# Memory cross-attention of an encoder layer: token and probability tiles split before the transposition, and transposed by DMA instead of by TensorE

## The chip, the cores and the metric

The kernel runs on one core of a Trainium2 chip, as one launch. The metric is the device time of that core in microseconds (us), the median over several executions. The core has five engines with instruction queues of their own: TensorE (PE in the profile; its weight loads are PEld), VectorE (DVE), ScalarE (ACT), GpSimd (POOL) and SyncE (SP, whose queue here issues almost all DMA transfers).

## The reference

One post-norm encoder layer over 1024 tokens of width 1024: a token mixer (an mLSTM in both directions beside a two-dimensional neighbourhood attention), a cross-attention into 256 memory tokens, and a gated convolutional feed-forward block, each followed by a residual sum and a layer norm. The change lies in the cross-attention alone:

```
def memory_xattn(x, mem, w_q, w_kv, w_o, b_o):
    q = (x @ w_q).reshape(b, t, 4, 256)
    k, v = split(mem @ w_kv)                      # 256 memory tokens, 4 heads x 256
    s = einsum('bthd,bmhd->bhtm', q, k) * 256 ** -0.5
    p = softmax(s, axis=-1)
    o = einsum('bhtm,bmhd->bthd', p, v).reshape(b, t, d)
    return o @ w_o + b_o
h = layer_norm(ALPHA * h + memory_xattn(h, ...), ln2_w, ln2_b)
```

## The kernel before

All large products are made of three float16 products. An operand is scaled by a power of two and written as a pair hi + lo, where hi is its value rounded to float16 and lo is the float16 of what is left. `split16` (L203 to L205) makes such a pair: ScalarE writes hi (L204) and VectorE writes lo (L205). `mm3` (L224 to L227) then issues hi x hi, hi x lo and lo x hi into the same PSUM bank, as lines L225, L226 and L227.

The weights of the cross-attention are folded early in the kernel: w_q with the keys of each head becomes `Kq` (1024 x 1024: token width by 4 heads x 256 memory tokens), and the values of each head with w_o become `Vo` (1024 x 1024). So a tile of 128 tokens needs two products of 128 x 1024 x 1024. Both contract over the partition axis, so the left operand of each has to be turned from token-major (tokens on the partitions) to token-minor (tokens along the row).

The 1024 tokens are eight tiles of 128, taken in the order of the list `todo`. The stages around the change are:

- The output projection of the mixer (`out_half`, with `after1`, L1296 to L1307) ends with layer norm 1 of each tile. Its tiles are stored to `h1_d` in DRAM (L1300). Here the first two tiles are already transposed for the attention (`to_hT` at L1304 and L1306).
- `to_hT` (L1265 to L1271) takes a tile `r`, a 128 x 1024 float32 array. TensorE transposes its eight 128 x 128 blocks, four to a PSUM bank (L1270), and `split16` evicts each bank as a pair of 128 x 512 into `h1T`.
- `scores` (L1386 to L1407) multiplies `h1T` with `Kq` (48 matmuls of 128 x 512), takes the row maximum of each head (L1396, L1397), the exponential with its row sum (L1400), the reciprocal (L1403), and multiplies the probabilities of each head with it in place (L1405). There is one buffer `P` of 128 x 1024 float32.
- `to_PT` (L1409 to L1418) transposes the eight blocks of `P` by TensorE (L1416) and evicts them with `split16` into a float16 pair. These pairs live in the tiles `vec0`, `vec1`, `vec2` of the pool `vecs`; `vec0` and `vec1` held the weight and the bias of layer norm 1 before (L1298 reads `vec0`, L1299 reads `vec1`).
- `out_d` (L1420 to L1435) multiplies the probabilities with `Vo` (48 matmuls), adds the residual (L1428), normalises, stores the tile to `h2_d` (L1431), and calls `to_B`, which transposes the tile once more by TensorE (L1332) for the feed-forward block. `to_B` is not touched by the change.

The loop at L1442 to L1451 runs `scores(n + 1)`, `to_PT(n)`, the load of tile n + 2 from `h1_d` (L1384), `to_hT(n + 2)`, and `out_d(n - 1)`. GpSimd adds the bias `b_xo` to tile n + 2 in place (L1449), after the tile's transposition has read it. The last three tiles' `out_d` is interleaved with the preparation of the first feed-forward weights (L1555 to L1578), whose loads (L1487) go into buffers that take the memory of the attention's work pool `ck` when that is closed (L1453).

Each engine runs its own instructions in a fixed order, SP's queue too: an instruction that waits holds all that stand behind it on the same engine. That order is fixed when the program is built, by a scheduler that works with estimated durations (`schedule_with_timeline_sim=True`). It is not simply the order of the source: in the trace the transpositions of one tile lie between matmuls of another.

Of the kernel before, what the change touches and what calls it, by code (L numbers as in the profile page):

```python
# [11 lines left out]
F16 = mybir.dt.float16  # L12
I32 = mybir.dt.int32
AF = mybir.ActivationFunctionType
OP = mybir.AluOpType
PSUM = bass.MemoryType.PSUM

D = 1024
# [38 lines left out]
def encoder(ctx, tc, I, out):  # L57
    nc = tc.nc
    V, A, G, T, S = nc.vector, nc.scalar, nc.gpsimd, nc.tensor, nc.sync
# [25 lines left out]
    def tbank():  # L85
        return pp.tile([128, 512], F32, name="tp", tag="tp", bufs=2).rearrange("p (k t) -> p k t", k=4)
# [17 lines left out]
    ident = consts.tile([128, 128], F32, name="ident")  # L104
# [98 lines left out]
    def split16(hi, lo, src, s):  # L203
        A.activation(hi, src, AF.Copy, scale=s)  # L204
        return V.scalar_tensor_tensor(lo, src, s, hi, op0=OP.mult, op1=OP.subtract)  # L205
# [76 lines left out]
    with ExitStack() as ca:  # L282
# [819 lines left out]
        with ExitStack() as cn:  # L1102
# [4 lines left out]
            o = 0  # L1107
# [27 lines left out]
            def na_gen():  # L1135
                n = 0
                for p in range(4):
# [15 lines left out]
                    for cb in range(4):  # L1153
# [26 lines left out]
                        for g in range(4):  # L1180
# [4 lines left out]
                                kl[:, r0:r0 + R, :].rearrange("p r c -> p (r c)"), True, True)  # L1185
                            P = nw.tile([128, 384], F32, name="P", tag="P", bufs=5)
                            mn = nw.tile([128, 2], F32, name="mn", bufs=6)
                            V.tensor_tensor_reduce(P[:, :nk], ps, tabs[ct, rt].rearrange("p r c -> p (r c)"), 1.0, BIG,
                                                   OP.add, OP.min, mn[:, 0:1])
                            A.activation(P[:, :nk], P[:, :nk], AF.Exp, scale=-1.0, bias=mn[:, 0:1],  # L1190
                                         accum_out=mn[:, 1:2])
                            V.reciprocal(mn[:, 1:2], mn[:, 1:2])
                            V.tensor_scalar(P[:, :nk], P[:, :nk], mn[:, 1:2], None, op0=OP.mult)
                            yield 1
# [38 lines left out]
    with ExitStack() as cb_:  # L1233
# [27 lines left out]
        rs, hT, probs, rq, holds, stores = {}, {}, {}, [], [], []  # L1261
        cC = ExitStack()
        ck = cC.enter_context(tc.tile_pool(name="wkC", bufs=1, reuse_waits="tile"))

        def to_hT(ck, n, r):  # L1265
            hT[n] = ck.tile([128, 2, 8, 128], F16, name="h1T", tag="h1T", bufs=2)
            for q in range(2):
                pt = tbank()
                for k in range(4):
                    T.transpose(pt[:, k, :], r[:, (4 * q + k) * 128:(4 * q + k + 1) * 128], ident)  # L1270
                split16(hT[n][:, 0, 4 * q:4 * q + 4], hT[n][:, 1, 4 * q:4 * q + 4], pt, s1)  # L1271

        with ExitStack() as cB:
            wk = cB.enter_context(tc.tile_pool(name="wkB", bufs=1, reuse_waits="tile"))
            lw, lb = vec(0, "ln1_w"), vec(1, "ln1_b")
            p1, s1 = pow2(ln_bound(lw, lb)[1], 14)
# [109 lines left out]
        def scores(ck, n):  # L1386
            t = hT.pop(n)
            P = ck.tile([128, D], F32, name="P", tag="P", bufs=1)
            mn = small.tile([128, 8], F32, name="mn", bufs=3)
            for ch in range(2):  # L1390
                ps = bank("S2")
                for k in range(8):
                    c = slice(ch * 512, ch * 512 + 512)
                    mm3(ps, t[:, 0, k], t[:, 1, k], Kq[0][:, k, c], Kq[1][:, k, c], k == 0, k == 7)
                m = mn[:, 2 * ch:2 * ch + 2]
                V.tensor_reduce(m, ps.rearrange("p (h m) -> p h m", h=2), axis=mybir.AxisListType.X, op=OP.max)  # L1396
                V.tensor_scalar(m, m, ncs, None, op0=OP.mult)  # L1397
                for h in range(2 * ch, 2 * ch + 2):
                    o = h % 2 * 256
                    A.activation(P[:, h * 256:h * 256 + 256], ps[:, o:o + 256], AF.Exp, scale=cs_, bias=mn[:, h:h + 1],  # L1400
                                 accum_out=mn[:, 4 + h:5 + h])
                l = mn[:, 4 + 2 * ch:6 + 2 * ch]
                V.reciprocal(l, l)  # L1403
                for h in range(2 * ch, 2 * ch + 2):
                    V.tensor_scalar(P[:, h * 256:h * 256 + 256], P[:, h * 256:h * 256 + 256], mn[:, 4 + h:5 + h], None,  # L1405
                                    op0=OP.mult)
            return P  # L1407

        def to_PT(P, n):  # L1409
            i = 2 if n == NT - 1 else n % 2  # L1410
            t = f16(vecs.tile([128, D], F32, name=f"vec{i}", tag=f"vec{i}")).rearrange(
                "p (n k t) -> p n k t", n=2, k=8)
            for q in range(2):
                pt = tbank()
                for k in range(4):
                    T.transpose(pt[:, k, :], P[:, (4 * q + k) * 128:(4 * q + k + 1) * 128], ident)  # L1416
                split16(t[:, 0, 4 * q:4 * q + 4], t[:, 1, 4 * q:4 * q + 4], pt, 2.0 ** 14)
            probs[n] = t  # L1418

        def out_d(n, lag=1):  # L1420
# [20 lines left out]
        P = scores(ck, 0)  # L1441
        for n in range(NT - 1):  # L1442
            Pn = scores(ck, n + 1)
            to_PT(P, n)
            P = Pn
# [4 lines left out]
            if 0 < n < NT - 2:  # L1450
                run(out_d(n - 1))  # L1451
        to_PT(P, NT - 1)
        cC.close()  # L1453

# [143 lines left out]
        with ExitStack() as cE:  # L1598
# [113 lines left out]
            for v in range(NFF):  # L1712
# [25 lines left out]
                if v == NFF - 2:  # L1738
                    y_scale(0)
                    s1 = sy[0][1]  # L1740
# [41 lines left out]
        with ExitStack() as cF:  # L1782
# [49 lines left out]
            for tt in range(NT):  # L1832
                load_r(tt + 2)
                r = rs.pop(tt)
# [8 lines left out]
                n = 256 if last else 512  # L1843
# [95 lines left out]
```

## Time and profile before

| | us |
|---|---|
| median of 3 runs | 1519.65 |
| lowest and highest | 1518.59, 1522.79 |
| span of the profiled execution | 1519.5 |
| PE busy | 1457.8 (96%) |
| DVE busy | 1030.0 (68%) |
| ACT busy | 821.2 (54%) |
| POOL busy | 570.6 (38%) |
| attention stage (first scores to last `out_d` matmul) | 669.7 to 858.1 |

The profiled execution has no other time than its span. It is 0.15 us below the median. The page groups instructions by source line, so L225, L226 and L227 stand for the three products of all matmuls that go through `mm3`; the names beside them (`S<-kq,h1T` for the scores, `S<-whi,vec` and `S<-wlo,vec` for `out_d`) tell which product it is. A matmul's row gives its full duration, but matmuls overlap: the time that one takes away from the next is the distance between their starts.

### The profile page before, as it was taken

How to read it: one execution, taken by the hardware profiler on the slowest of the kernel's cores; microseconds unless marked ns; L12 is line 12 of the kernel's file. 1: busy time of each engine (PE TensorE's matmuls, PEld its weight loads, DVE VectorE, ACT ScalarE, POOL GpSimd, SP SyncE). 2: the span in 40 equal slices, each digit the busy share in tenths (PEclk: the TensorE clock that was granted, in tenths of full speed). 3: DMA queues.
4: the chain of work that ended last, by engine and by line, in shares of the span. 5: the costliest groups of instructions: out<-in, count | busy, mean ns of one | idle time of the engine just before them, and what ended most of it. 6: DMA issues, size and time to landing. Idle time of an engine off the chain costs nothing.

```text
span 1519.5 us, 21884 instructions
## 1 busy us (share of the span) xinstructions
PE 1457.8 (96%) x8188; PEld 881.0 (58%) x8188; DVE 1030.0 (68%) x1953; ACT 821.2 (54%) x1385; POOL 570.6 (38%) x453
## 2 busy tenths in 40 slices
PE   8999999999999898998999989999999999999998
PEld 7998766456766887864555434444444444444444
DVE  7868766536677678575357778887787779707434
ACT  5766565655544666333245767777777767503000
POOL 5442357303325765043112364444443420300543
PEclk9999999999999999999999989999999999999999
DMA  8846653215545533553011242223222436712121
GB/s 305 326 156 211 189 190 120 91 54 144 155 118 180 196 124 131 213 194 125 29 42 60 96 152 112 111 111 125 111 111 111 152 125 222 276 43 89 51 82 56
DMA packets 84895, 208.61 MB, mean 137 GB/s; under 512 B 7091, under 2 KB 36019, under 8 KB 81462
## 3 DMA queue, kind: packets, MB, share of 16 engines
q1 hardware_dynamic: 84496, 206.46, 39.2%
q8 instruction: 64, 1.05, 0.3%
q0 software_dynamic: 144, 0.49, 0.2%
q14 instruction: 41, 0.34, 0.1%
q10 hardware_dynamic: 150, 0.27, 0.0%
HBM read 158.34 MB, written 49.35 MB: 137 GB/s over the span
## 4 chain that ended last, share of the span: by engine, by line
PE 48%; DVE 18%; ACT 9%; DMA 9%; issue 4%; POOL 2%; SPq 1%; DVEq 0%; ACTq 0%; POOLq 0%
PE dn L225 5%; PE dn L227 5%; PE dn L226 5%; DMA sv<-in_w_down_dram 5%; PE S L225 3%; PE S L227 3%; PE S L226 3%; DVE wlo L205 3%; DVE cbuf L1617 3%; DVE cbuf L1618 2%; PE cl L225 2%; PE cl L226 2%; PE cl L227 2%; PE cu L227 1%; PE o L1202 1%
## 5 line engine op out<-in xcount | busy, mean ns | idle before, releaser
L1529 POOL TENSOR_TENSOR wraw<-ur 128x512 f32<-128x512 f32 x22 | 46.3, 2105 | 201.0 <-issue 193.6
L226 PE MATMUL dn<-wlo,yp 128*128 128x512 f16 (+1 forms) x284 | 105.1, 370 | 0.0
L225 PE MATMUL dn<-whi,yp 128*128 128x512 f16 (+1 forms) x284 | 104.9, 370 | 0.0
L227 PE MATMUL dn<-whi,yp 128*128 128x512 f16 (+1 forms) x284 | 104.4, 370 | 0.0
L1617 DVE SCALAR_TENSOR_TENSOR cbuf<-C,wdw,cbuf 128x1024 f32<-128x1024 f32 x44 | 69.8, 1585 | 34.8 <-ACT cbuf L1616 34.6
L227 PEld LDWEIGHTS <-wlo 128*128 128x128 f16 x540 | 52.8, 98 | 56.7 <-DVE wlo L205 1.3
L226 PEld LDWEIGHTS <-whi 128*128 128x128 f16 x540 | 52.9, 98 | 55.9 <-issue 3.2
L225 PEld LDWEIGHTS <-whi 128*128 128x128 f16 x540 | 52.8, 98 | 56.1 <-ACT whi L204 3.6
L253 ACT ACTIVATE r<-r,lnrs 128x1024 f32<-128x1024 f32 x19 | 23.6, 1242 | 100.3 <-DVE lnrs L252 100.3
L205 DVE SCALAR_TENSOR_TENSOR wlo<-wraw,us,whi 128x1024 f16<-128x1024 f32 (+1 forms) x48 | 61.6, 1302 | 18.5 <-ACT whi L204 18.5
L1618 DVE SCALAR_TENSOR_TENSOR cbuf<-C,wdw,cbuf 128x1024 f32<-128x1024 f32 x44 | 71.2, 1618 | 0.9
L1616 ACT ACTIVATE cbuf<-C,bdw,wdw 128x1024 f32<-128x1024 f32 x44 | 54.1, 1234 | 10.2 <-DVE C L1654 9.6
L204 ACT ACTIVATE whi<-wraw,us 128x1024 f16<-128x1024 f32 (+1 forms) x48 | 51.2, 1103 | 15.4 <-DVE us L177 14.8
L226 PEld LDWEIGHTS <-yp 128*128 128x128 f16 x370 | 36.2, 98 | 39.9
L225 PEld LDWEIGHTS <-yp 128*128 128x128 f16 x370 | 36.2, 98 | 39.8
L227 PEld LDWEIGHTS <-yp 128*128 128x128 f16 x370 | 36.2, 98 | 39.7
L243 POOL TENSOR_TENSOR lnrs<-lnrs,mhalf 128x1 f32<-128x1 f32 x32 | 23.9, 746 | 90.9 <-DVE lnrs L242 85.2
L225 PE MATMUL tk<-whi,Bo 128*128 128x256 f16 (+1 forms) x192 | 53.3, 278 | 1.9 <-DVE stage L205 1.9
L227 PE MATMUL tk<-whi,Bo 128*128 128x256 f16 (+1 forms) x192 | 53.4, 278 | 0.0
L225 PE MATMUL tk<-whi,Be 128*128 128x256 f16 (+1 forms) x192 | 52.6, 274 | 0.8 <-DVE stage L205 0.8
L226 PE MATMUL tk<-wlo,Bo 128*128 128x256 f16 (+1 forms) x192 | 53.3, 277 | 0.0
L226 PE MATMUL tk<-wlo,Be 128*128 128x256 f16 (+1 forms) x192 | 52.4, 274 | 0.9 <-DVE wlo L205 0.9
(524 smaller groups left out, 4911.8 us busy)
## 6 DMA issues: line engine op xcount, KB each, us to landing
ur<-in_w_up_dram SPq DMA_DIRECT2D x22, 1024.0 KB
sv<-in_w_down_dram SPq DMA_DIRECT2D x22, 512.0 KB
y<-cbuf SPq DMA_DIRECT2D x22, 512.0 KB
ur<-y SPq DMA_DIRECT2D x11, 1024.0 KB
wraw<-in_w_down_dram SPq DMA_DIRECT2D x22, 512.0 KB
r<-h SPq DMA_DIRECT2D x19, 512.0 KB
h<-r SPq DMA_DIRECT2D x16, 512.0 KB
wraw<-in_w_tok_dram SPq DMA_DIRECT2D x10, 512.0 KB
```

The lines of the kernel that those rows point to most:

```text
L204: A.activation(hi, src, AF.Copy, scale=s)
L205: return V.scalar_tensor_tensor(lo, src, s, hi, op0=OP.mult, op1=OP.subtract)
L225: T.matmul(ps, lh, rh, start=first, stop=False, skip_group_check=skip)
L226: T.matmul(ps, lh, rl, start=False, stop=False, skip_group_check=skip)
L227: return T.matmul(ps, ll, rh, start=False, stop=last, skip_group_check=skip)
L243: G.tensor_tensor(rs[:, 0:1], rs[:, 0:1], mhalf[:, 0:1], OP.pow)
L253: A.activation(r, r, AF.Identity, scale=rs[:, 0:1], bias=rs[:, 1:2])
L1202: anchor[0] = T.matmul(po[:, g, :], vt[:, r0 // 4 + b, :], PT[:, b, :], start=b == 0, stop=b == nb - 1)
L1529: G.tensor_tensor(S1, A21, A22, OP.add)
L1616: A.activation(c, C[:, 1:SEQ + 1], AF.Identity, scale=wdw[:, 1, j:j + 1], bias=bdw[:, j:j + 1])
L1617: V.scalar_tensor_tensor(c, C[:, 0:SEQ], wdw[:, 0, j:j + 1], c, op0=OP.mult, op1=OP.add)
L1618: V.scalar_tensor_tensor(c, C[:, 2:SEQ + 2], wdw[:, 2, j:j + 1], c, op0=OP.mult, op1=OP.add)
```

## The change

`to_hT` no longer uses TensorE. It splits the tile token-major (128 x 1024, one `split16` out of SBUF) into a new buffer `h1s`, and two DMA transposes on SP's queue, one of the hi and one of the lo array (128 x 1024 float16 each, 256 KB), write `h1T`. In `scores` the reciprocal is multiplied by 2^14, and `split16` with that factor replaces the multiplication L1405: it writes hi and lo of each head token-major into a new buffer `Ps`. `to_PT` is then only two DMA transposes on SP's queue. Both new buffers have two copies of 4 KB per partition.

```
         def to_hT(ck, n, r):
             hT[n] = ck.tile([128, 2, 8, 128], F16, name="h1T", tag="h1T", bufs=2)
-            for q in range(2):
-                pt = tbank()
-                for k in range(4):
-                    T.transpose(pt[:, k, :], r[:, (4 * q + k) * 128:(4 * q + k + 1) * 128], ident)
-                split16(hT[n][:, 0, 4 * q:4 * q + 4], hT[n][:, 1, 4 * q:4 * q + 4], pt, s1)
+            hl = ck.tile([128, 2, D], F16, name="h1s", tag="h1s", bufs=2)
+            split16(hl[:, 0], hl[:, 1], r, s1)
+            for i in range(2):
+                S.dma_start_transpose(hT[n][:, i], hl[:, i])
...
         def scores(ck, n):
             t = hT.pop(n)
             P = ck.tile([128, D], F32, name="P", tag="P", bufs=1)
+            hl = ck.tile([128, 2, D], F16, name="Ps", tag="Ps", bufs=2)
...
                 V.reciprocal(l, l)
+                V.tensor_scalar(l, l, 2.0 ** 14, None, op0=OP.mult)
                 for h in range(2 * ch, 2 * ch + 2):
-                    V.tensor_scalar(P[:, h * 256:h * 256 + 256], P[:, h * 256:h * 256 + 256], mn[:, 4 + h:5 + h], None,
-                                    op0=OP.mult)
-            return P
-
-        def to_PT(P, n):
+                    o = slice(h * 256, h * 256 + 256)
+                    split16(hl[:, 0, o], hl[:, 1, o], P[:, o], mn[:, 4 + h:5 + h])
+            return hl
+
+        def to_PT(hl, n):
             i = 2 if n == NT - 1 else n % 2
             t = f16(vecs.tile([128, D], F32, name=f"vec{i}", tag=f"vec{i}")).rearrange(
                 "p (n k t) -> p n k t", n=2, k=8)
-            for q in range(2):
-                pt = tbank()
-                for k in range(4):
-                    T.transpose(pt[:, k, :], P[:, (4 * q + k) * 128:(4 * q + k + 1) * 128], ident)
-                split16(t[:, 0, 4 * q:4 * q + 4], t[:, 1, 4 * q:4 * q + 4], pt, 2.0 ** 14)
+            for i in range(2):
+                S.dma_start_transpose(t[:, i], hl[:, i])
             probs[n] = t
```

## The prediction

> **What bounds the kernel now.** I read the busy times of stretches first, with the attention stage cut into its start (669 to 726 us), two ordinary tiles, and the head of the feed-forward block.
>
> ```profile
> core 0: us, PE busy (x) PEld busy (x) DVE busy (x) ACT busy (x) POOL busy (x), PEclk, DMA share, GB/s
> 669.00:704.00 35.00, 33.12 (x158) 15.39 (x157) 22.29 (x46) 10.64 (x22) 19.02 (x11) 1.00 0.66 248
> 704.00:726.00 22.00, 19.82 (x103) 10.01 (x102) 8.51 (x20) 6.86 (x15) 3.32 (x3) 1.00 0.06 24
> 758.00:780.00 22.00, 22.00 (x115) 11.43 (x114) 11.05 (x25) 9.24 (x21) 2.86 (x2) 1.00 0.15 49
> 780.00:802.00 22.00, 22.00 (x115) 11.49 (x114) 15.25 (x30) 11.10 (x24) 5.97 (x4) 1.00 0.12 41
> 871.00:890.00 19.00, 12.57 (x43) 4.74 (x43) 16.87 (x20) 12.37 (x16) 16.96 (x22) 0.73 0.39 139
> ```
>
> From 758 to 802 PE is busy all 44 us at a granted clock of 1.00, DVE at most 15.25 of 22, ACT 11.10, and the DMA engines are nearly idle (0.15 and 0.12). There TensorE alone sets the pace, so PE time taken out is time gained. At the start of the stage that doesn't hold: PE is idle for 1.88 of 35 us and 2.18 of 22 us. The waits of PE from 690 to 722 us are these:
>
> ```profile
> PE S L227 <- DVE vec L205: 1.3, 1, 1.3
> PE tp L1270 <- DVE vec L205: 1.0, 1, 1.0
> PE S L225 <- ACT P L1400: 0.8, 1, 0.8
> PE S L225 <- ACT vec L204: 0.6, 1, 0.6
> PE S L225 <- ACT h1T L204: 0.4, 1, 0.4
> ```
>
> All five hang on the transpositions: evictions out of the transposed banks, and a softmax that had to wait until `P` was transposed. They sum to 4.1 us.
>
> **What a TensorE transposition costs.** Not its duration but the distance to the next matmul counts, from the time line of PE:
>
> ```profile
> 757.49 0.38 PE L227 MATMUL S<-kq,h1T 128*128 128x512 f16 x1
> 757.70 1.04 PE L1416 MATMUL tp<-ident,P 128*128 128x128 f32 x8
> 758.58 0.38 PE L227 MATMUL S<-whi,vec 128*128 128x512 f16 x1
> ```
>
> Eight blocks take 758.58 - 757.70 = 0.88 us, 0.11 us each; a 128x512 matmul takes 757.70 - 757.49 = 0.21 to 0.22 us (its 0.38 is overlap). The change removes 8 tiles x 2 x 8 = 128 blocks, at most 128 x 0.11 = 14.1 us. With the 4.1 us of waits the gain cannot pass 18.2 us, 1501.3 of the span of 1519.5.
>
> How many of these blocks lie where PE is the bound? After 719 us the blocks of `tp` are
>
> ```profile
> L1416 PE MATMUL tp<-ident,P x48: 272/273/273, 729.6 to 833.5; 128*128 128x128 f32 x48
> L1332 PE MATMUL tp<-ident,r x44: 272/272/281, 747.3 to 849.9; 128*128 128x128 f32 x44
> L1270 PE MATMUL tp<-ident,r x36: 272/273/273, 724.9 to 811.0; 128*128 128x128 f32 x36
> ```
>
> of which L1332 stays: 48 + 36 = 84 blocks go, 84 x 0.11 = 9.2 us. The other 44 lie in the start, which needs its own working.
>
> **What the change puts in their place.** Thirty-two DMA transposes of 256 KB, four a tile. The trace of before has none, so I bound them by its transfers out of or into SBUF, as the chain of waits gives them:
>
> ```profile
> 193.47 6.80 DMA kq<-stage
> ...
> 407.37 3.27 DMA whi<-mrow
> ...
> 473.56 2.57 DMA nqk<-ev
> ```
> ```profile
> whi<-mrow SPq DMA_DIRECT2D x16, 256.0 KB
> nqk<-ev SPq DMA_DIRECT2D x16, 256.0 KB
> ```
>
> Same size, plain layout: 2.57 and 3.27 us. A larger transfer beside other traffic: 6.80. I take 3.0 us to landing, nearest to the two of the same size, and 1 us more for the second of a pair; the upper end for the range is 6.80. [...]
>
> In the ordinary tiles this latency is hidden: the tokens of tile n + 2 are wanted after all 48 matmuls of `out_d(n - 1)` (48 x 0.216 = 10.4 us), the probabilities of tile n after 48 matmuls of the scores of n + 2. A pair with its split needs about 2.4 + 4 us. If that cover were gone, each pair would cost up to 6.4 us.
>
> The splits change little. The rows of VectorE from 690 to 850 us, shortest, median and longest in ns:
>
> ```profile
> L205 DVE SCALAR_TENSOR_TENSOR vec<-tp,vec x16: 678/686/692, 693.6 to 834.4; 128x512 f16<-128x512 f32 x16
> L205 DVE SCALAR_TENSOR_TENSOR h1T<-tp,sc,h1T x12: 696/748/752, 705.5 to 812.0; 128x512 f16<-128x512 f32 x12
> ...
> L205 DVE SCALAR_TENSOR_TENSOR unitYh<-wraw,us,unitYh x1: 1232/1232/1232, 849.8 to 849.8; 128x1024 f16<-128x1024 f32 x1
> ```
> ```profile
> L1405 DVE TENSOR_SCALAR P<-P,mn x28: 335/349/356, 694.5 to 828.6; 128x256 f32<-128x256 f32 x28
> ```
>
> Per tile DVE spends 4 x 0.349 + 2 x 0.686 + 2 x 0.748 = 4.26 us on this. After: one 128x1024 split, 1.23, four of 128x256 at about 0.37 (half a 512 one, an estimate), 1.48, and two tiny multiplications, at most 0.35 each as the smallest of these rows: 3.4 us. DVE gets about 0.8 us a tile lighter; ACT, whose four 256-wide pieces replace two 512-wide ones, about as busy as before. I cost both at nothing: PE hides them.
>
> The change adds a wait on SP's queue. Each transpose waits for a split, and behind it stand the load of the next tile (L1384), the store of `h2_d` (L1431) and at the end the first feed-forward weights (L1487). Nobody waits closely for the store; the load has a buffer of five tiles. The danger is the start.
>
> **The start, step by step.** The rows, from the time lines of DVE, SP and PE:
>
> ```profile
> 690.06 1.23 DVE L1298 TENSOR_TENSOR r<-r,vec 128x1024 f32<-128x1024 f32 x1 [1.31 <-ACT r L253]
> ```
> ```profile
> 693.73 0.32 SPq L1300 DMA_DIRECT2D h<-r  x1
> 694.15 2.72 SPq L1384 DMA_DIRECT2D r<-h  x5
> ```
> ```profile
> 690.43 1.04 PE L1416 MATMUL tp<-ident,P 128*128 128x128 f32 x8
> 692.02 0.39 PE L225 MATMUL S<-whi,vec 128*128 128x512 f16 x1 [0.56 <-ACT vec L204]
> ```
> ```profile
> 703.89 1.04 PE L1270 MATMUL tp<-ident,r 128*128 128x128 f32 x8
> 705.33 0.39 PE L225 MATMUL S<-kq,h1T 128*128 128x512 f16 x1 [0.40 <-ACT h1T L204]
> ```
> ```profile
> 715.78 1.04 PE L1416 MATMUL tp<-ident,P 128*128 128x128 f32 x8
> 717.79 0.66 PE L1270 MATMUL tp<-ident,r 128*128 128x128 f32 x4 [0.98 <-DVE vec L205]
> 719.25 0.38 PE L225 MATMUL S<-whi,vec 128*128 128x512 f16 x1 [0.80 <-ACT P L1400]
> ```
>
> The first probabilities go into `vec0`, which L1298 reads until 690.06 + 1.23 = 691.3. That gate is DVE's, so the 16 blocks of tiles 0 and 1, which PE did earlier (1.8 us), buy nothing. Before, the product with `Vo` began at 692.02 and ended at 703.89. After, the transposes are issued at 691.3 at the earliest and the hi array lands at 691.3 + 0.3 (an issue, as L1300) + 3.0 = 694.6; lo, 1 us later, comes as the third product needs it. `out_d(0)` ends at 694.6 + 10.4 = 705.0, 1.1 us late. Tile 2 is the third of five loads issued from 694.15; all have landed by 704 (the DMA share falls from 0.66 to 0.06), so the third by about 701. With ACT's hi (1.2), an issue and a transpose it is there at 705.5, lo about a microsecond later with 0.3 us of waiting: the scores of tile 2 start at 705.5 instead of 705.33 and end at 716.3. Then the gain begins: `out_d(1)` started at 719.25, behind twelve transpositions and two waits, and can start at 716.3, 2.9 us earlier.
>
> **The sum.** 2.9 + 9.2 = 12.1 us at the end of the attention. What follows is not PE's: from 871 to 890 PE is idle for 6.43 of 19 us behind the last `to_B` and the first weights. Their inputs come earlier with the attention, so most passes through; between 0 and 6.4 us I give back 1.5, near nothing because DVE's own work there follows the attention's end. Gain 10.6 us: 1508.9 on the profiled execution's span of 1519.5, which lies 0.15 below the median; 1509.0 on the median. About 0.3%, 4.6 us, is what a measurement of this kernel can tell from no change.
>
> **The rivals.** First, the start is blocked by SP's order (0.13). If the first probabilities' transposes stand behind the five loads, they land after those, at 704 + 1.5 at best. `out_d(0)` then ends at 715.9, the scores of tile 2 at 726.3 instead of 715.78, and `out_d(1)` begins 7.1 us late. Against that the 9.2 us remain, less 1.5: 1518.9. For it speaks that these loads were held until the last store at 693.73, so SP's order there is tight; against, that the probabilities' gate opens 2.4 us earlier than that store. A TensorE gap of 12 us could also lower the clock: in 871 to 890 it was 0.73 after PE had idled, and 43 matmuls took 12.57 us instead of 43 x 0.216 = 9.3, 3.3 us; with that it is 1522.
>
> Second, another wait takes half the gain in the ordinary tiles (0.15): the store of `h2_d`, which waits for a layer norm, stands ahead of a needed transpose, or DVE, at 15.25 of 22 us, hands over late. Then 9.2 becomes 4.6 and the time is 1513.6.
>
> Third, on the slower side: the transposes run one after another and set the pace (0.10). A tile takes 48 + 48 matmuls; from one set of eight L1416 blocks at 757.70 to the next it is 22.3 us, and 22.3 - 16 x 0.11 = 20.5 us without the blocks:
>
> ```profile
> 779.96 1.04 PE L1416 MATMUL tp<-ident,P 128*128 128x128 f32 x8
> ```
>
> Four transposes that can't overlap set the pace from 20.5 / 4 = 5.1 us each and lose from 22.3 / 4 = 5.6. At the 6.80 of the longest row it is 27.2 us a tile, 4.9 more over six tiles, 29 us, and the first pair lands at 691.3 + 13.6 = 704.9 instead of 692.0, 13 us: about 1562. Against it: 3 us is what the same size took, and the DMA engines are idle here. [...]
>
> **How the numbers follow.** Forecast 0.62 at 1509.0, and the rivals 0.13, 0.15 and 0.10. Faster by over 0.3%: the forecast and the second rival, 0.77, less 0.01 for a second rival that is worse: 0.76. Within 0.3%: the first rival, 0.13. Slower: the third, with the first one's clock case, 0.11. The range runs from 1504, where the start loses none of its waits' 4.1 us and nothing is given back, to 1520, which takes in the first rival and leaves out the third.
>
> **What would show it.** Right: no L1270 or L1416 on PE; from 758 to 802 PE still full, with a tile every 20.5 us; a gap of PE of about 5 us before the first product with `Vo`; no PE wait on a DMA of `h1T` or `vec` afterwards; transposes landing in 2.5 to 3.5 us. Wrong: a PE wait on such a DMA in every tile, a DMA share far above 0.15 in the ordinary tiles, a clock below 1.00 there, or SP with a transpose behind a store.

## The result, and the profile after

The changed kernel takes 1526.2 us (median of 5 runs, 1524.32 to 1526.25) against 1519.65 (1517.44 to 1522.79) for the kernel before on the same chip: a ratio of 1.0036, with a 95% interval of 1.0023 to 1.0049. It is slower. Forecast was 1509.0, with a range to 1520. The profiled execution took 1526.06 us in all, 1.96 more than its span of 1524.1; the prediction had counted the span of before as the whole execution. Span against span the change costs 1524.1 - 1519.5 = 4.6 us, between the medians 6.55. All times and ratios below are of fast runs: two of the ten executions of e9 took 2518.61 and 5341.35 us and are left out.

First the page's lines on the span and the engines:

```profile
span 1524.1 us, 21708 instructions
PE 1447.8 (95%) x8060; PEld 869.3 (57%) x8060; DVE 1033.7 (68%) x1945; ACT 825.6 (54%) x1393; POOL 574.5 (38%) x453
```

The change was made: PE has 128 matmuls fewer (8060, from 8188) and 10.0 us less work (1447.8, from 1457.8). Yet the span is longer, so PE must stand idle for some 14.6 us more. The stretches say where; they are those that the prediction showed of before:

```profile
core 0: us, PE busy (x) PEld busy (x) DVE busy (x) ACT busy (x) POOL busy (x), PEclk, DMA share, GB/s
669.00:704.00 35.00, 19.38 (x89) 8.56 (x88) 27.27 (x50) 13.54 (x29) 13.92 (x9) 0.84 0.51 182
704.00:726.00 22.00, 18.40 (x72) 7.39 (x71) 8.82 (x10) 4.69 (x4) 13.99 (x6) 0.87 0.82 208
758.00:780.00 22.00, 22.00 (x107) 10.49 (x106) 11.81 (x25) 9.73 (x22) 2.89 (x2) 1.00 0.45 83
780.00:802.00 22.00, 22.00 (x107) 10.48 (x106) 13.32 (x28) 11.64 (x25) 4.99 (x3) 1.00 0.38 102
```

The ordinary tiles (758 to 802) are as forecast: PE full, clock 1.00, 8 instructions fewer in each 22 us. The DMA share has risen from 0.15 and 0.12 to 0.45 and 0.38, and PE stays full. The start is another matter: in 669 to 704 PE works 19.38 us instead of 33.12. The waits of PE from 640 to 900 us (sum, times, longest) hold one entry that explains nearly all of it:

```profile
PE S L225 <- DMA vec<-Ps: 15.6, 1, 15.6
PE z L226 <- DVE us L176: 3.7, 1, 3.7
...
PE S L225 <- DMA h1T<-h1s: 2.4, 1, 2.4
...
PE S L227 <- DMA h1T<-h1s: 1.2, 1, 1.2
```

`vec<-Ps` are the first probabilities' transposes. No wait on a transpose comes back after 720 us. How the one wait arises is seen on VectorE, which carries most of layer norm 1: statistics (L238), their aggregation, the variance's offset (L242), then GpSimd's inverse root (L243), VectorE's shift (L252), ScalarE's scaling (L253). The lines that follow are one lower in the changed kernel: L1297 multiplies with the norm's weight in `vec0`, L1298 (GpSimd) adds its bias, L1299 stores. These are the norms' last steps on the time line of DVE (start, duration, ending with the idle time before it and its releaser):

```profile
683.24 1.23 DVE L1297 TENSOR_TENSOR r<-r,vec 128x1024 f32<-128x1024 f32 x1
684.39 0.15 DVE L242 TENSOR_SCALAR lnrs<-lnmv 128x1 f32<-128x1 f32 x1
...
688.53 0.20 DVE L252 TENSOR_SCALAR lnrs<-lnmv,lnrs 128x1 f32<-128x1 f32 x1
...
696.02 0.21 DVE L252 TENSOR_SCALAR lnrs<-lnmv,lnrs 128x1 f32<-128x1 f32 x1
...
698.57 1.23 DVE L1297 TENSOR_TENSOR r<-r,vec 128x1024 f32<-128x1024 f32 x1 [0.76 <-ACT r L253]
```

The last multiplication ends at 698.57 + 1.23 = 699.8. I call this the gate: until then `vec0` is taken and the first probabilities have no place to land. In the kernel before it was 691.3. SP's and PE's time lines go on from there:

```profile
699.83 2.60 SPq L1415 DMA_TRANSPOSE vec<-Ps  x2
702.52 0.53 SPq L1299 DMA_DIRECT2D h<-r  x1
703.15 3.19 SPq L1415 DMA_TRANSPOSE vec<-Ps  x2
706.44 2.75 SPq L1383 DMA_DIRECT2D r<-h  x5
```
```profile
703.07 0.61 PE L225 MATMUL S<-whi,vec 128*128 128x512 f16 x1 [15.62 <-DMA vec<-Ps]
717.58 0.39 PE L225 MATMUL S<-kq,h1T 128*128 128x512 f16 x1 [2.40 <-DMA h1T<-h1s]
860.48 0.38 PE L227 MATMUL S<-whi,vec 128*128 128x512 f16 x1
```

The transposes go out 0.03 us after the gate opens, and the product with `Vo` begins 3.24 us later. Behind them on SP stand the last store of `h1`, the second probabilities, and only then the five loads (706.44, before 694.15), so tile 2's tokens are late as well. The scores of tile 2 start at 717.58 instead of 705.33, **12.25 us late**. From there to the last matmul of the attention it is 860.48 - 717.58 = 142.9 us, before 857.88 - 705.33 = 152.6 (its last one):

```profile
857.88 0.38 PE L227 MATMUL S<-whi,vec 128*128 128x512 f16 x1
```

So the tiles win **9.65 us**, the start loses 12.25, and the attention ends 2.6 us late. The remaining 2.0 us of the span lie behind it, above all at the head of the feed-forward block, where a wait on a split before L226 is 3.7 us instead of 1.6.

### The profile page after: what moved, and what is told of

It is laid out like the page before. It is cut to its first block, busy times and chain, and to the rows that moved or that the text cites. A ratio compares the mean times of both kernels' runs of the same rounds, so it can differ in the third digit from the quotient of the medians.

```text
span 1524.1 us, 21708 instructions
## 1 busy us (share of the span) xinstructions
PE 1447.8 (95%) x8060; PEld 869.3 (57%) x8060; DVE 1033.7 (68%) x1945; ACT 825.6 (54%) x1393; POOL 574.5 (38%) x453
## 5 line engine op out<-in xcount | busy, mean ns | idle before, releaser
L226 PE MATMUL dn<-wlo,yp 128*128 128x512 f16 (+1 forms) x284 | 105.1, 370 | 0.0
L226 PEld LDWEIGHTS <-whi 128*128 128x128 f16 x540 | 52.9, 98 | 56.0 <-issue 3.2
L243 POOL TENSOR_TENSOR lnrs<-lnrs,mhalf 128x1 f32<-128x1 f32 x32 | 24.8, 775 | 138.5 <-DVE lnrs L242 132.8
L253 ACT ACTIVATE r<-r,lnrs 128x1024 f32<-128x1024 f32 x19 | 23.6, 1240 | 88.1 <-DVE lnrs L252 88.0
L225 PE MATMUL S<-whi,vec 128*128 128x512 f16 x128 | 49.3, 385 | 15.6 <-DMA vec<-Ps 15.6
L204 ACT ACTIVATE whi<-wraw,us 128x1024 f16<-128x1024 f32 (+1 forms) x48 | 51.2, 1103 | 16.5 <-DVE us L177 15.6
L226 PEld LDWEIGHTS <-yp 128*128 128x128 f16 x370 | 36.2, 98 | 39.9
L226 PE MATMUL tk<-wlo,Bo 128*128 128x256 f16 (+1 forms) x192 | 53.3, 278 | 0.0
L226 PE MATMUL tk<-wlo,Be 128*128 128x256 f16 (+1 forms) x192 | 52.4, 274 | 0.9 <-DVE wlo L205 0.9
```

What stands on the lines that cost most here:

```text
L225: T.matmul(ps, lh, rh, start=first, stop=False, skip_group_check=skip)
L226: T.matmul(ps, lh, rl, start=False, stop=False, skip_group_check=skip)
L243: G.tensor_tensor(rs[:, 0:1], rs[:, 0:1], mhalf[:, 0:1], OP.pow)
L253: A.activation(r, r, AF.Identity, scale=rs[:, 0:1], bias=rs[:, 1:2])
```

## The experiments

Landmarks of all kernels, each from its profiled execution: the gate; the first product with `Vo`; the first scores of tile 2; the start of the last matmul of the attention; and the ratio of the times to the kernel before with its 95% interval. For a kernel whose first probabilities go by TensorE the gate is the same multiplication's end.

| kernel | gate | first `Vo` | tile 2 | last | ratio |
|---|---|---|---|---|---|
| before | 691.3 | 692.0 | 705.3 | 857.9 | 1 |
| after | 699.8 | 703.1 | 717.6 | 860.5 | 1.0036 [1.0023, 1.0049] |
| e1 first tokens by TensorE | 692.1 | 695.5 | 711.8 | 853.8 | 0.9969 [0.9956, 0.9981] |
| e2 first tokens and probabilities by TensorE | 690.3 | 691.0 | 705.0 | 845.7 | 0.9946 [0.9929, 0.9962] |
| e3 all tokens by TensorE | 690.4 | 693.8 | 707.7 | 853.1 | 0.9994 [0.9984, 1.0004] |
| e4 all probabilities by TensorE | 698.5 | 699.1 | 714.9 | 864.9 | 1.0062 [1.0047, 1.0077] |
| e5 loads of `Vo` later | 702.3 | 705.5 | 719.8 | 862.7 | 1.0029 [1.0016, 1.0041] |
| e6 transposed twice in four tiles | 698.4 | 701.7 | 716.3 | 859.2 | 1.0024 [1.0012, 1.0036] |
| e7 PE kept running | 698.1 | 701.4 | 716.2 | 860.3 | 1.0011 [1.0002, 1.0020] |
| e8 first transposes on ScalarE's queue | 697.3 | 700.8 | 715.8 | 856.4 | 1.0006 [0.9994, 1.0017] |
| e9 bias on VectorE | 691.2 | 694.6 | 709.8 | 851.3 | 0.9987 [0.9975, 0.9998] |
| e11 = e2 with e9 | 688.4 | 690.9 | 702.1 | 843.1 | 0.9916 [0.9899, 0.9934] |
| e12 before with e9 | 685.9 | 687.8 | 699.0 | 853.2 | 0.9960 [0.9943, 0.9978] |
| e13 = e2, tile 2's tokens too | 689.1 | 690.0 | 703.2 | 844.7 | 0.9914 [0.9892, 0.9936] |
| e14 = e1 with unread splits and transposes | 701.6 | 704.9 | 719.2 | 863.8 | 1.0037 [1.0024, 1.0050] |
| e15 = e1 with unread splits | 697.7 | 701.1 | 715.5 | 860.9 | 1.0018 [1.0007, 1.0029] |

Between the last attention matmul and the end of the span lie 657.7 us (e12) to 664.0 (e6), though nothing was changed there: the waits at the feed-forward's head and on its evictions come out differently in each kernel. So where the question is the attention, the landmarks are the sharper measure; the ratios carry a few us of that.

### Which part of the change costs: e1 to e4

In e1 only the tokens of tiles 0 and 1 go back to TensorE:

```
             hT[n] = ck.tile([128, 2, 8, 128], F16, name="h1T", tag="h1T", bufs=2)
+            if n < 2:
+                for q in range(2):
+                    pt = tbank()
+                    for k in range(4):
+                        T.transpose(pt[:, k, :], r[:, (4 * q + k) * 128:(4 * q + k + 1) * 128], ident)
+                    split16(hT[n][:, 0, 4 * q:4 * q + 4], hT[n][:, 1, 4 * q:4 * q + 4], pt, s1)
+                return
             hl = ck.tile([128, 2, D], F16, name="h1s", tag="h1s", bufs=2)
```

> Undo one part: the token tiles 0 and 1, those transposed during the mixer's output projection, go through TensorE as before the change; the other 28 transposes stay on DMA. Theory (the two early token transposes hold SP's queue, so the last mixer tiles are loaded and normalised about 8 us late, and the first probabilities' tile comes free that much later): the last read of the layer norm weight ends near 691 instead of 699.8, the wait of PE for the first probabilities falls from 15.6 to 3 to 6 us, and the time is about 1515 (1512 to 1518). Rival (DMA transposes cost time in every tile, by contention or by the splits): nothing much changes, 1524 to 1527.

Measured: 1516.58 us, ratio 0.9969. These two tiles alone turn a loss of 0.36% into a gain of 0.31%, a swing of 0.67%, 10 us. The gate is back at 690.89 + 1.23 = 692.1, and the wait on the first probabilities falls from 15.6 to 4.8:

```profile
690.89 1.23 DVE L1304 TENSOR_TENSOR r<-r,vec 128x1024 f32<-128x1024 f32 x1 [0.92 <-ACT r L253]
```
```profile
PE S L225 <- DMA vec<-Ps: 4.8, 1, 4.8
PE S L225 <- DMA h1T<-h1s: 3.7, 1, 3.7
```

So the way in which tokens are made that PE wants at 667 us decides whether `vec0` comes free at 692 or at 700.

In e2 the probabilities of tiles 0 and 1 go back to TensorE as well (with the old multiplication in `scores`); the other six tiles stay with DMA:

```
-            hl = ck.tile([128, 2, D], F16, name="Ps", tag="Ps", bufs=2)
+            hl = None if n < 2 else ck.tile([128, 2, D], F16, name="Ps", tag="Ps", bufs=2)
...
-            for i in range(2):
-                S.dma_start_transpose(t[:, i], hl[:, i])
+            if n < 2:
+                for q in range(2):
+                    pt = tbank()
+                    for k in range(4):
+                        T.transpose(pt[:, k, :], hl[:, (4 * q + k) * 128:(4 * q + k + 1) * 128], ident)
+                    split16(t[:, 0, 4 * q:4 * q + 4], t[:, 1, 4 * q:4 * q + 4], pt, 2.0 ** 14)
+            else:
+                for i in range(2):
+                    S.dma_start_transpose(t[:, i], hl[:, i])
```

> The start as before the change: tokens and probabilities of tiles 0 and 1 through TensorE, the other 24 transposes on DMA. Theory (all the loss lies in the start): PE waits under 6 us from 669 to 726, no clock drop, 96 blocks of 0.11 us saved, less some microseconds for tile 2's tokens: about 1511 (1508 to 1514), below the kernel before. Rival (loss in every tile): above 1519.

Measured: 1511.81 us, ratio 0.9946, faster than both kernels. The start is that of before (tile 2 at 705.0), and PE's rows show that the tiles then bring what they should:

```profile
705.04 0.39 PE L225 MATMUL S<-kq,h1T 128*128 128x512 f16 x1 [1.11 <-DMA h1T<-h1s]
845.69 0.38 PE L227 MATMUL S<-whi,vec 128*128 128x512 f16 x1
```

The attention ends 857.88 - 845.69 = 12.2 us earlier. The prediction's sum for this point was 12.1.

e3 and e4 undo one half in all tiles: in e3 all tokens are transposed by TensorE and all probabilities by DMA (e1's branch with `if True`), in e4 the reverse (e2's second branch, for all tiles).

> One part alone: probabilities by DMA, all tokens through TensorE. Theory: the mixer is undisturbed, the first probabilities land near 694.5 instead of being ready at 692; 64 blocks saved, 7 us, less 3 to 4: about 1516 (1513 to 1518). Rival (the probabilities' latency with nothing to fill it is the whole cause): the wait stays above 10 us, 1522 to 1526.

> The other part alone: tokens by DMA, all probabilities through TensorE. Theory: the mixer's last tiles are late as in the changed kernel, the product with the values starts about 8 us late and the clock falls a little; 7 us are saved: about 1521 (1518 to 1524). Rival (the probabilities' latency is the whole cause): the start is undisturbed and 64 blocks are saved, 1511 to 1514.

Measured: 1519.35 us, ratio 0.9994, for e3; 1529.51 us, ratio 1.0062, for e4. Both are slower than I had expected. From 758 to 780 us PE is busy all the time, with 112 instructions in e3 and 111 in e4, between the 115 of before and the 107 of the changed kernel: each half pays in the ordinary tiles. From tile 2's scores to the last matmul e3 needs 145.4 us and e4 150.0, where before needs 152.6 and after 142.9; e4 has in that stretch a wait of 2.4 us on the second half of tile 2's tokens, and from 718.7 to 722.5 us its matmuls start 0.43 us apart instead of 0.21 to 0.22. At the start they differ: e3, without early token transposes, has the gate at 690.4, e4 has it at 698.5. The early tokens are the harmful part, and in e4 they harm a kernel whose probabilities never see a DMA.

### What in the early tokens: e5 to e8

e5 tests whether the loads of `Vo` stand ahead of the mixer's last load on SP: they are issued after it.

```
-                S.dma_start(rs[tt], res[tt * 128:(tt + 1) * 128, :])
+                part_ld[0] = S.dma_start(rs[tt], res[tt * 128:(tt + 1) * 128, :])
...
-                S.dma_start(v_, vo_d[n, :, 2 * i:2 * i + 2])
+                with tc.issue_after(part_ld[0].ins):
+                    S.dma_start(v_, vo_d[n, :, 2 * i:2 * i + 2])
```

> All 32 transposes as in the changed kernel, but the loads of the folded values (vo, 4 MB) are issued only after the last load of the mixer's part tiles. Theory (the last part tile lands at 679.5 instead of 670.8 because five of the value loads stand before it, and that delay is what reaches the first probabilities): it lands near 671, the last read of the norm's weight ends at 692 to 695, the time is about 1519 (1516 to 1522). Rival (the delay comes from the order of the norms and softmaxes on VectorE and GpSimd, not from the load): the last read stays near 699, 1524 to 1528.

Measured: 1525.51 us, ratio 1.0029, no different from the changed kernel. In e5 the last load of the mixer goes out ahead of all loads of `Vo`, and still the gate opens at 702.3. The order behind those loads is not the cause; that theory fell.

e6 transposes the probabilities of tiles 2 to 5 a second time into the same place, eight more DMA transposes of 256 KB.

```
             for i in range(2):
                 S.dma_start_transpose(t[:, i], hl[:, i])
+                if 2 <= n <= 5:
+                    S.dma_start_transpose(t[:, i], hl[:, i])
```

> The changed kernel with the probabilities of tiles 2 to 5 transposed twice, the second time onto the first: 8 more DMA transposes, 40 in all, in the ordinary tiles; the output is the same. Theory (the transposes of the ordinary tiles are hidden behind PE): no PE wait in those tiles, 1525 to 1528 like the changed kernel. Rival (they cost by contention or by holding SP's queue): 0.7 us or more for each added one, 1532 or more.

Measured: 1525.02 us, ratio 1.0024. From tile 2's scores to the end of the attention it is 859.18 - 716.26 = 142.9 us, as without the extra eight, though the DMA share of an ordinary tile has risen from 0.45 to 0.56:

```profile
758.00:780.00 22.00, 22.00 (x107) 10.51 (x106) 12.47 (x24) 10.14 (x25) 2.90 (x2) 1.00 0.56 106
```

In the ordinary tiles the transposes are hidden with room to spare.

e7 fills PE's gap ahead of the first probabilities with 64 matmuls whose result nobody reads, to see what the lower clock costs.

```
-                    mm3(ps, t[:, 0, k], t[:, 1, k], Kq[0][:, k, c], Kq[1][:, k, c], k == 0, k == 7)
+                    last_s[0] = mm3(ps, t[:, 0, k], t[:, 1, k], Kq[0][:, k, c], Kq[1][:, k, c], k == 0, k == 7)
...
+            if n == 0:
+                warm = tbank().rearrange("p k t -> p (k t)")
+                with tc.issue_after(last_s[0].ins):
+                    for i in range(64):
+                        T.matmul(warm, Kq[0][:, 0, :128], Kq[0][:, 1, :512], start=True, stop=True)
```

> The changed kernel with 64 matmuls of 128x512 on unused values after the scores of tile 1, whose result nobody reads: they fill 13.8 us of the gap of PE before the first product with the values, and add nothing else. Theory (the granted clock falls because PE idles, and that costs about 3.6 us on top of the waits): the clock stays 1.00 from 669 to 714, the first product takes 10.4 instead of 12.1 us, the time is 1522 to 1524. Rival (the lower clock costs nothing that isn't waiting anyway): 1525 to 1528.

Measured: 1523.51 us, ratio 1.0011, but the landmarks deny that the clock's part is won back. `out_d(0)` does run at full clock (1.00 from 703 to 712 us), yet after the next gap, 3.5 us ahead of tile 2's tokens, the clock is lower again, now for longer (0.50 from 719 to 722 us and 0.61 from 722 to 725), and the attention ends at 860.3 as in the changed kernel. The better time comes from the feed-forward block, where e7 has 7.9 us of PE waits after 900 us and the changed kernel 10.4; that is no answer to the question asked.

e8 issues the four early token transposes from ScalarE's queue, so that nothing on SP stands behind them.

```
-                S.dma_start_transpose(hT[n][:, i], hl[:, i])
+                (A if n < 2 else S).dma_start_transpose(hT[n][:, i], hl[:, i])
```

> All 32 transposes, but the four of token tiles 0 and 1 are issued from ScalarE's queue, so that SP's queue doesn't wait for their splits; ScalarE spends some 1.3 us on each issue. Theory (holding SP's queue is the harm): the part loads go out as before the change, the gate of the first probabilities opens at 692 to 695, 1515 to 1520. Rival (the transposes themselves disturb the mixer's traffic, whoever issues them): 1524 to 1528.

Measured: 1521.82 us, ratio 1.0006. SP's time lines, the changed kernel first, then e8:

```profile
649.75 0.32 SPq L1299 DMA_DIRECT2D h<-r  x1
650.93 3.19 SPq L1270 DMA_TRANSPOSE h1T<-h1s  x2
654.22 0.53 SPq L1071 DMA_DIRECT2D r<-part  x1
657.17 0.32 SPq L1299 DMA_DIRECT2D h<-r  x1
658.35 4.70 SPq L1270 DMA_TRANSPOSE h1T<-h1s  x2
663.14 0.53 SPq L1071 DMA_DIRECT2D r<-part  x1
```
```profile
650.08 0.32 SPq L1299 DMA_DIRECT2D h<-r  x1
653.23 0.32 SPq L1071 DMA_DIRECT2D r<-part  x1
657.50 0.32 SPq L1299 DMA_DIRECT2D h<-r  x1
661.21 0.32 SPq L1071 DMA_DIRECT2D r<-part  x1
```

A load of the mixer's last partial sums follows the store by 4.47 and 5.97 us in the changed kernel, by 3.15 and 3.71 in e8: the transposes hold it by 1.3 and 2.3 us. Against the kernel before they hold it by less, 0.5 and 1.7 us: there it follows by 3.96 and 4.25 us (store at 651.17, load at 655.13; store at 657.45, load at 661.70). The gate moves from 699.8 to 697.3, the end of the attention from 860.5 to 856.4. A part, but only a part.

### Is it the gate? e9 and e12

In e9 the bias additions of the last four tiles' norms, 2.35 us each on GpSimd, are made by VectorE, on top of the changed kernel; e12 makes the same edit in the kernel before.

```
-                G.tensor_tensor(r, r, lb, OP.add)
+                (V if tt in todo[4:] else G).tensor_tensor(r, r, lb, OP.add)
```

> The changed kernel, with the bias addition of layer norm 1 (L1298) on VectorE instead of GpSimd for the last four tiles. Theory: the chain of the last norms, at 7.5 us a step, opens the gate of vec0 late, and a part of each step is GpSimd's power standing behind a bias addition of 2.35 us. Then the gate comes 3 to 7 us earlier than 699.8 (693 to 697), the TensorE wait on the first probabilities falls from 15.6 to 9 to 13 us, and the time is 1517 to 1522. Rival (VectorE's own order holds the chain, GpSimd's additions cost nothing): VectorE has four more operations of about 1.2 us, the gate stays at 700 or goes later, and the time is 1525 to 1529.

> The kernel before, with the same bias additions on VectorE: the control for the run above. Theory: there the norms' steps near the end are already short (3.8 us in one of them, because the power is issued ahead of the bias addition), and TensorE has little waiting there, so the time stays within 1518 to 1522. Rival (the addition on GpSimd costs both kernels alike): 1513 to 1517.

Measured: e9 1519.2 us, ratio 0.9987; e12 1515.38 us, ratio 0.9960. The gate of e9 is at 689.95 + 1.22 = 691.2:

```profile
689.95 1.22 DVE L1297 TENSOR_TENSOR r<-r,vec 128x1024 f32<-128x1024 f32 x1 [0.38 <-ACT r L253]
```

It opens 8.6 us earlier than in the changed kernel, more than I expected, and the ratio falls by 0.49%, 7.4 us. In e12 the gate opens 5.4 us earlier than before (685.9), and the ratio falls by 0.40%, 6.1 us. My theory for the control was wrong: the norms' chain sets the start in the kernel before, too. Both runs together say that the gate's time passes into the kernel's nearly one to one; e9 does not say that GpSimd's additions are what the change made worse, since both kernels win by the edit.

### Combining: e11 and e13

e11 is e2 with e9's edit; e13 is e2 with the tokens of tile 2 by TensorE too (`if n < 3` in `to_hT`).

> Tokens and probabilities of tiles 0 and 1 by TensorE, the other six tiles by DMA, and the last four bias additions on VectorE. Theory: with the start by TensorE the norms' chain is no longer what TensorE waits for, so the additions bring at most 1 us beside the kernel without them (1511.8): 1510 to 1513. Rival (any lightening of the chain is gained): 1506 to 1509.

> Tokens of tiles 0, 1 and 2 and probabilities of tiles 0 and 1 by TensorE, the rest by DMA. Theory: tile 2's tokens are the next that TensorE waits for at the start (1.5 us on them, 1.3 and 0.4 on evictions of the first probabilities, in the kernel with two tiles by TensorE); transposing tile 2 by TensorE removes that wait and adds 8 blocks of 0.11 us: between 1 us faster and 1 us slower than 1511.8. Rival (tile 2's tokens by DMA are hidden): 0.9 us slower, the blocks alone.

Measured: 1509.12 us, ratio 0.9916, and 1508.37 us, ratio 0.9914. e11 won more than my theory allowed: the attention ends 2.6 us earlier than in e2, so the chain was still on the path. In e13 the attention ends 1.0 us earlier than in e2, at the edge of what was expected; the rest of its lead of 3.4 us lies behind the attention and is not explained. Both are about 0.85% faster than the kernel before; e13 has the lowest median, but the intervals of the two overlap.

### Splits or transposes: e14 and e15

Both start from e1, where TensorE makes the first tokens. e15 adds, for tiles 0 and 1, a token-major split that nobody reads; e14 adds the split and two DMA transposes of it, unread as well.

```
             if n < 2:
+                a = ck.tile([128, 2, D], F16, name="h1s", tag="h1s", bufs=2)
+                split16(a[:, 0], a[:, 1], r, s1)
+                d = ck.tile([128, 2, D], F16, name="h1s", tag="h1s", bufs=2)
+                for i in range(2):
+                    S.dma_start_transpose(d[:, i].rearrange("p (k t) -> p k t", k=8), a[:, i])
                 for q in range(2):
```

> Tokens of tiles 0 and 1 by TensorE, as in the kernel that measured 1516.6 with its gate at 692.1, and beside it the same token-major splits and DMA transposes of these two tiles as in the changed kernel, with results that nobody reads. Theory: the splits (on ScalarE and VectorE between the steps of the norms) and the transposes (on SP's queue ahead of the stores and loads of the mixer's last tiles) are by themselves what delays the norms, whoever makes the tokens: the gate goes to 696 to 701 and the time to 1520 to 1526. Rival (what counts is that TensorE has no transpositions to do there, so that it runs ahead and the order of the engines is built differently): the gate stays at 691 to 694 and the time at 1516 to 1519.

> The same without the unread DMA transposes: only the two unread token-major splits are added. If the hold on SP's queue is the cause, the gate stays at 691 to 694 and the time at 1516 to 1519. If the splits on ScalarE and VectorE are, it goes to 695 to 701 and 1519 to 1526, as with the transposes. The changed kernel with its early transposes on ScalarE's queue (gate 697.3, 1521.8) says that both have a part: then it lies between, at 693 to 697.

Measured: e14 1526.96 us, ratio 1.0037; e15 1523.63 us, ratio 1.0018. The last multiplications with the norm's weight, e14 and then e15:

```profile
700.40 1.23 DVE L1309 TENSOR_TENSOR r<-r,vec 128x1024 f32<-128x1024 f32 x1 [1.22 <-ACT r L253]
```
```profile
696.44 1.21 DVE L1306 TENSOR_TENSOR r<-r,vec 128x1024 f32<-128x1024 f32 x1
```

From e1's 692.1 the splits alone move the gate to 697.7, by 5.5 us; the transposes move it by another 4.0, to 701.6. With TensorE doing all it did before for these tiles, the unread work costs what the change costs (1.0037 and 1.0036). So two early splits and four early DMA transposes are enough to delay the gate, and TensorE need not be freed for it. The gate of e15 lies a little above the 693 to 697 that I gave for the mixed case, and both the gate and the time of e14 a little above its ranges. But these runs do not divide the changed kernel's 8.5 us: here the unread splits come on top of the evictions of TensorE's transposes, while in the changed kernel a split of 1.27 us on VectorE and 1.15 on ScalarE stands in the place of two evictions of 1.41 and 1.27 us together (655.42 and 654.70 in the kernel before).

## Why the prediction was wrong, point by point

**The ordinary tiles: right.** 84 blocks at 0.11 us, 9.2 us, plus 2.9 from the first twelve blocks and the waits around them: 12.1 us at the end of the attention. With the start left to TensorE (e2) it was 12.2. The changed kernel itself won 9.65 us from tile 2's scores on.

**A transpose's latency: right.** 3.0 us after a short issue was taken, from the 2.57 and 3.27 us of plain transfers of the same size; 3.24 us passed from the issue to the first product. The 1 us more for the second of a pair was an estimate; in e7, where PE waited for both arrays of the first probabilities, it started on the lo array 702.61 - 701.39 = 1.2 us after the hi array:

```profile
701.39 0.39 PE L225 MATMUL S<-whi,vec 128*128 128x512 f16 x1 [1.71 <-DMA vec<-Ps]
702.61 0.39 PE L227 MATMUL S<-whi,vec 128*128 128x512 f16 x1 [0.61 <-DMA vec<-Ps]
```

**The transposes set the pace: rightly thought unlikely.** SP issues one per 1.27 us (the median of 16), and eight extra cost nothing (e6: 142.9 us from tile 2's scores to the last matmul with them and without). The eight blocks of a transpose are issued in 1.27 us, and those of the first hi array were in use 3.24 us after the start of the issue.

**The start: here it failed.** The step is the sentence "That gate is DVE's, so the 16 blocks of tiles 0 and 1, which PE did earlier (1.8 us), buy nothing", with the gate at "691.3", together with "I cost both at nothing", which was said of the work on VectorE and ScalarE. I read off the trace of before that the gate hangs on DVE, and then took its time over as a constant, though the change alters that very stretch: it puts two splits of 128x1024 on ScalarE and VectorE in the place of the evictions, and four transposes on SP ahead of loads that the mixer's last tiles need. The gate came at 699.8. Of these 8.5 us, e8 wins back 2.5 by taking the transposes off SP's queue. The other 6.0 I put down, from the time lines below, to where the splits stand in VectorE's order and to what follows from it; no run sets that alone.

How a split of 1.27 us can cost more than that is read in the time lines, not tested by itself. The second halves of the norms (L252) of the third and fourth tile, in the kernel before and then in the changed one:

```profile
657.96 0.21 DVE L252 TENSOR_SCALAR lnrs<-lnmv,lnrs 128x1 f32<-128x1 f32 x1 [1.13 <-POOL lnrs L243]
664.78 0.21 DVE L252 TENSOR_SCALAR lnrs<-lnmv,lnrs 128x1 f32<-128x1 f32 x1 [1.38 <-POOL lnrs L243]
```
```profile
651.60 1.27 DVE L205 SCALAR_TENSOR_TENSOR h1s<-r,sc,h1s 128x1024 f16<-128x1024 f32 x1
...
658.00 1.29 DVE L1090 TENSOR_TENSOR r<-out,r 128x512 f32<-128x512 f32 x2 [3.26 <-DMA r<-part]
659.20 0.20 DVE L252 TENSOR_SCALAR lnrs<-lnmv,lnrs 128x1 f32<-128x1 f32 x1
...
666.90 1.29 DVE L1090 TENSOR_TENSOR r<-out,r 128x512 f32<-128x512 f32 x2 [3.85 <-PE out L227]
668.11 0.20 DVE L252 TENSOR_SCALAR lnrs<-lnmv,lnrs 128x1 f32<-128x1 f32 x1
```

In these two steps of the kernel before, L252 waits only for GpSimd, and the evictions of the transposed tokens fill a part of that wait (655.42 and 661.99, behind L242). In the changed kernel the split stands between the norm's statistics and their aggregation, and evictions of the projection (L1090) stand ahead of L252 and wait 3.26 us for a load that SP held behind the transposes, and 3.85 us for PE. The step from the third to the fourth norm takes 8.9 us instead of 6.8. Near the end another 3.8 us go: before, one norm's step took 681.51 - 677.74 = 3.8 us, because the order had its L242 ahead of the weight multiplication, so that GpSimd made that norm's inverse root before it added the last tile's bias. In the changed kernel L1297 comes first (683.24, then L242 at 684.39), the addition of 2.35 us goes ahead, and the step takes 7.5. That order is the scheduler's.

The starts of L252 add up to the whole delay. In the changed kernel the first one comes 1.3 us earlier (644.44 instead of 645.78). From the second to the fourth it takes 17.8 us instead of 13.1, which loses 4.8. From the fourth to the sixth nothing is lost. From the sixth to the start of the last multiplication it takes 17.6 us instead of 12.3, another 5.3, and there no early split or transpose stands any more. That last stretch takes 15.3 to 17.6 us in the eight kernels with early token-major splits (after, e4 to e8, e14, e15) and 12.3 to 13.5 in the five without (before, e1, e2, e3, e13); of these the two with the first probabilities by DMA, e1 and e3, need the 13.5. So more than half of the delay arises behind the early splits and transposes, where VectorE's order has come out differently.

One thing in that order can be seen. Three tiny operations of the softmax on VectorE take about 2 us each in the changed kernel, ahead of the gate; in the kernel before, the only such one comes after the gate:

```profile
677.26 1.75 DVE L1397 TENSOR_SCALAR mn<-mn,sc 128x2 f32<-128x2 f32 x1
685.17 1.76 DVE L1397 TENSOR_SCALAR mn<-mn,sc 128x2 f32<-128x2 f32 x1
692.24 2.22 DVE L1404 TENSOR_SCALAR mn<-mn 128x2 f32<-128x2 f32 x1
```
```profile
691.92 1.81 DVE L1397 TENSOR_SCALAR mn<-mn,sc 128x2 f32<-128x2 f32 x1
```

Mostly these operations take 0.17 to 0.23 us, and the prediction had taken the new one, L1404, at 0.35 at most. Each of the four begins during a bias addition on GpSimd and ends within 0.03 us of its end (678.98, 686.90 and 694.43; before 693.71). In e9, where VectorE makes these additions, no such operation ahead of the gate takes more than 0.23 us. How much of the 5.1 us that the three take beyond the usual reaches the gate is open, since VectorE waits for other things behind them too; and no run sets the order alone, so the shares of the splits' place, the softmax and the additions stay open.

**The rivals.** The first one, the start blocked by SP's order, was nearest: for it I had 1518.9, and 1522 with the clock, and after the gap of 15.6 us the clock was 0.50 from 703 to 706, which cost `out_d(0)` 1.7 us. But its place was wrong. SP was blocked 50 us earlier, ahead of the mixer's loads, and the larger part was not SP's. The second rival (half the gain lost in the tiles) didn't come: no wait on a transpose after 720 us.

**Given back.** Between 0 and 6.4 us behind the attention were allowed for, 1.5 taken; 2.0 were lost. Since that stretch varies by several us between kernels that don't differ there, this says little.

**The range.** It ended at 1520, because the start's loss was bounded by the first rival. The bound should have come from the gate: had it been asked what 2 x 1.27 us and four transposes do to a chain of eight norms in series, a loss at the start of several us would have been a case of its own, and the sign open.

## What to carry to other kernels

A landmark that one reads from the trace of before is a constant only if the change adds or moves nothing ahead of it, on any engine or queue of the chain that leads to it; so follow that chain back past every place where the change adds or moves work. Work that moves off the bounding engine pays in the stretches where that engine bounds, and there alone: here five or six tiles by DMA and the first ones by TensorE beat the kernel before by 0.5 to 0.9%, while all eight by DMA lost. And when a control with the same edit also wins (e12), the edit has found a bound of both kernels, not the cause of the difference.

## What the runs showed of the hardware

The clock of PE after a gap. Stretches of the changed kernel around the first product with `Vo`:

```profile
691.00:695.00 4.00, 0.00 (x0) 0.00 (x0) 3.97 (x5) 1.46 (x6) 2.84 (x2) 0.71 0.01 2
695.00:699.00 4.00, 0.00 (x0) 0.00 (x0) 1.95 (x8) 3.25 (x9) 0.00 (x0) 0.50 0.32 131
703.00:706.00 3.00, 2.93 (x7) 1.04 (x8) 0.00 (x0) 0.00 (x0) 0.00 (x0) 0.50 1.07 282
706.00:709.00 3.00, 3.00 (x15) 1.34 (x14) 0.00 (x0) 0.00 (x0) 0.00 (x0) 0.95 0.96 225
720.00:723.00 3.00, 3.00 (x8) 1.06 (x7) 1.97 (x1) 1.00 (x1) 3.00 (x2) 0.50 1.16 119
```

PE's last matmul ahead of the gap ends at 687.45. The granted clock is 1.00 until nearly 693 (0.82 from 692 to 693), some 5 us into the gap, then 0.50, and stays at 0.50 for about 3 us after work has come back (7 matmuls in 3 us, then 15). After gaps of 2.4 and 1.2 us on tile 2's tokens, with four matmuls between them, it was lower again, with a delay: 0.50 from 720 to 723, while PE worked. In both stretches the matmuls start 0.43 us apart instead of 0.216, so that about half the length is lost: `out_d(0)` spans 12.1 us, 703.07 to 715.18, where 48 x 0.216 = 10.4 would do.

A DMA transpose of 256 KB occupied SP's queue for 1.27 us (the median of the 16 of L1415, 1.23 to 1.56), four times the 0.32 of a plain store of `h1` (L1299 at 649.75). And tiny operations on VectorE can be long while GpSimd adds a 128x1024 bias: the multiplication of 128x2 numbers at 692.24 in the changed kernel took 2.22 us, 0.17 at 697.64, and ended with the addition (692.09 to 694.43).
